# One half unit of the output projection moves behind the projection's last part

## The chip, the cores and the metric

The kernel runs on one core of one Trainium2 chip. The metric is the device time of one execution in microseconds (us), lower is better. Five engines work side by side, each through its own instructions in its own order: PE (TensorE, matmuls; PEld are its weight loads), DVE (VectorE), ACT (ScalarE), POOL (GpSimd) and SP (SyncE, which here only issues DMAs). They wait for each other through semaphores.

## What is computed

The reference is one step of a hybrid streaming encoder over 576 tokens (64 of a sample, 512 of a prompt) with a model width of 1024:

```
h   = x @ W_in                                  # q, k, v of 8 + 8 heads, and an indexer
mix = concat(ForgettingAttention(h_A), IndexedSparseAttention(h_B))
x   = LN1(alpha * x + mix @ W_o)
x   = LN2(alpha * x + relu(x @ W_up)^2 @ W_down)
x   = x + sigmoid(x @ W_g + b_g) * (p @ W_ple)
```

The change lies in the third line, `alpha * x + mix @ W_o` and the LN1 behind it. `mix` has 1024 rows (features), 128 for each of eight pairs of heads.

## The kernel before

Everything is kept with the features on the 128 partitions and the 576 tokens along the free dimension. The tokens are worked in two halves of 288, called A and B. Each fp32 product is made from three matmuls of 32-bit words that were split into a high and a low part (`gemm`, L282 to L292): 128x128 weights by 128x288 data, three for each block of 128 input rows. `BH` and `BL` hold the high and low parts of `mix`, and after LN1 those of its result.

**Stages around the change, in program order.** `wo1` (L1117) multiplies `mix` by `W_o` for pairs 0 to 5 (768 of the 1024 rows): eight units, one for each 128 output features, each with both halves: 18 matmuls (6 blocks by 3) for a half. While it runs, the attention of pairs 6 and 7 is still being made; its small steps come from a second generator, `ticks`, and `drive(wo1(), 46, ticks(9 + 7), 48)` deals them out: 48 small steps over the first 46 of 48 yields, a yield being 6 matmuls. The result of each unit goes to `Y` by one DVE instruction (L1135: `Y*ALPHA + product`). Then `wo2(A)` (L1306) adds what is missing, pairs 6 and 7, for half A: 48 matmuls, in four steps of two output blocks each; DVE adds each step to `Y` (L1335) and `ln.add` sums `Y` over the features for LN1 of half A. `wo2(B)` does the same for half B, another 48, but first copies `Y` into the accumulator with ACT (L1313), and takes the sum back with ACT (L1333). `ple` follows: 96 matmuls on data of its own (`pT`), evacuated by ACT (L1350). Then `up_first` multiplies LN1's result by `W_up`, half A first.

**LN1** (class `LayerNorm`) is a chain over three engines that is dealt out between these matmuls: DVE and POOL sum `Y` (L1186 to L1191; for half A all on DVE, for half B the adds of the second and third step on POOL and the last on DVE), PE forms the mean (L1208 for A, L1206 for B), DVE subtracts it (L1232, four pieces), ACT squares (L1234, L1237), DVE adds the squares (L1238, L1240), PE forms the variance (L1258 for A), ACT and DVE take its inverse root, PE spreads it (L68), and DVE and ACT scale and split into `BH` and `BL` (L1270, L1274, L1278).

**Weights** arrive by SP's DMAs in fp32 (`wraw`, four places in this stage), ACT casts the high part (L191), DVE subtracts to get the low part (L195); both go to `whl`, 6 places until `wo1` is over and 13 from then on. A place is free again after the last matmul that reads it. `WT.ahead(u)` forces a unit's pieces to be made at that point of the program; `unit_w(u, oldest)` says which units still hold their places.

**Order.** A scheduler places the program's instructions on each engine's list at build time. On the chip each list is worked through in order, so the order on the list is what the change moves.

**PSUM.** The accumulators `m` and `g` of these stages rotate through three places (`psum_g`, two in one pool and one in another). A place is reused when its evacuation has read it.

Of the kernel before, what the change touches and what calls it, by code (L numbers as in the profile page):

```python
# [11 lines left out]
OP = mybir.AluOpType  # L12
# [12 lines left out]
ALPHA = 2.0 ** 0.25  # L25
# [6 lines left out]
HW = NT // 2  # L32
# [4 lines left out]
def tile_hybrid_step(ctx: ExitStack, tc: tile.TileContext, I, O):  # L37
    nc = tc.nc
    PE, ACT, DVE, POOL, SP = nc.tensor, nc.scalar, nc.vector, nc.gpsimd, nc.sync
# [34 lines left out]
    def later(delay, fn):  # L74
        evq.append((clock[0] + delay, len(evq), fn))
# [16 lines left out]
    def drive(main, n_main, bg, n_bg, drain=True, close=True):  # L92
        done = 0
        for i, _ in enumerate(main):
            clock[0] += 1
            pop_due(POP)
            for fl in fillers:
                fl()
            while bg is not None and done * n_main < (i + 1) * n_bg:
                done += 1  # L100
                if next(bg, 0) == 0:
                    bg = None
                    break
        if close:
            flush()
        if bg is not None and drain:
            for _ in bg:
                pass
# [171 lines left out]
    WT = Weights()  # L280

    def gemm(ps, W, kmap, aH, aL, cols, yield_every=6, first=True, last=True, wc=slice(0, 128), k0=0, onto=False):  # L282

        n = len(kmap) * 3
        i = 0
        for kw, ka in enumerate(kmap, k0):
            for w, a in ((0, aH), (0, aL), (1, aH)):
                PE.matmul(ps, W(w, kw, wc), a[:, ka, cols], start=(first and i == 0 and not onto), stop=(last and i == n - 1),  # L288
                          skip_group_check=onto)
                i += 1  # L290
                if i % yield_every == 0:
                    yield 1  # L292
# [47 lines left out]
    U = {}  # L340
# [506 lines left out]
    def proj(p):  # L847
# [4 lines left out]
        for kind in "kqv" if p else "qv":  # L852
            u = U[kind, p]
            W = WT.use(u)
            WT.ahead(u + 1)
# [5 lines left out]
            for h in range(2):  # L861
                for _ in gemm(m[:, h, :HW], W, range(8), AH, AL, slice(h * HW, (h + 1) * HW)):
                    WT.step()
# [6 lines left out]
    BH = BL = None  # L870
# [139 lines left out]
    def job(t):  # L1010
        return all_jobs[t] if 0 <= t < len(all_jobs) else None

    def ticks(n):

        for _ in range(n):
            t = tick_no[0]
            tick_no[0] += 1
            for micro in PLAN:
                for stage, lag in micro:
                    for x in (1, 0) if stage in LATE else (0,):  # L1020
                        j = job(t - lag - x)
                        if not j or (stage in LATE and j["late"] != x):
                            continue
                        if (j["close"] or stage not in (pv, oevac)) and not (stage is make_bias and "bias" in j):
                            stage(j)
                yield 1
# [65 lines left out]
    for p in range(7):  # L1092
# [5 lines left out]
        if p == 5:  # L1098
            Y = base.tile([128, 8, NT], F32, name="Y", tag="Y")
# [17 lines left out]
    def wo1():  # L1117
        side = delayed(7, v_out(7))
        for j in range(8):
            u = U["o", j]  # L1120
            W = WT.use(u)
            WT.ahead(u + 1)
            m = psum_m()
            for h in range(2):
                if (j, h) == (7, 1):
                    WT.ahead(u + 2)
                for _ in gemm(m[:, h, :HW], W, range(6), BH, BL, slice(h * HW, (h + 1) * HW)):
                    WT.step()
                    if j < 3:
                        next(side, 0)  # L1130
                    yield 1
                if j in (5, 6) and h == 0:
                    p_split(j - 5)
            y = Y[:, j].rearrange("p (a c) -> p a c", a=2)
            later(0, lambda y=y, m=m: DVE.scalar_tensor_tensor(  # L1135
                y, y, ALPHA, m[:, :, :HW], op0=OP.mult, op1=OP.add))

    drive(wo1(), 46, ticks(9 + 7), 48)
    pPA.close()
    pA.close()  # L1140

# [9 lines left out]
    A, B = slice(0, HW), slice(HW, NT)  # L1151
# [4 lines left out]
    def psum_g():  # L1156
        turn[0] += 1
        if turn[0] % 3 == 2:
            return psB.tile([128, 2, 512], F32, name="g", tag="g", bufs=1)
        return psM.tile([128, 2, 512], F32, name="g", tag="m", bufs=2)  # L1160
# [4 lines left out]
    unit_w = WT.use  # L1165

    class LayerNorm:
# [54 lines left out]
        def steps(self):  # L1222
# [80 lines left out]
            for j in range(0, 8, 2):  # L1303
                bias(j)
                yield 1

    def wo2(hs, ln, steps):
        onto = hs is B

        def take(j):  # L1310
            m = psum_g()
            if onto:
                ACT.copy(m[:, :, :HW], Y[:, j:j + 2, hs])  # L1313
            return m

        ms = {0: take(0)}
        for j in range(0, 8, 2):
            m = ms[j]
            if onto and j < 6:
                ms[j + 2] = take(j + 2)  # L1320
            for x in range(2):
                cs = slice((j + x) * 128, (j + x + 1) * 128)
                for k in (6, 7):
                    W = unit_w(U["ok", k], U["ok", 6])
                    for _ in gemm(m[:, x, :HW], W, (0,), BH[:, k:k + 1], BL[:, k:k + 1], hs,
                                  first=(k == 6), last=(k == 7), wc=cs, onto=onto):
                        pass
                WT.step(steps)
                yield 1

            def ev(j=j, m=m):
                if onto:
                    ACT.copy(Y[:, j:j + 2, hs], m[:, :, :HW])  # L1333
                else:
                    DVE.tensor_tensor(Y[:, j:j + 2, hs], m[:, :, :HW], Y[:, j:j + 2, hs], OP.add)  # L1335
                ln.add(j)
            later(0, ev)
            if not onto and j < 6:
                ms[j + 2] = take(j + 2)

    def ple():
        for j in range(8):
            W = unit_w(U["ple", j // 4])
            m = psum_g()
            for h in range(2):
                for _ in gemm(m[:, h, :HW], W, (0, 1), PT2[:, :, 0], PT2[:, :, 1], slice(h * HW, (h + 1) * HW),
                              wc=slice((j % 4) * 128, (j % 4 + 1) * 128)):
                    WT.step(j >= 4)
                    yield 1
            later(0, lambda j=j, m=m: ACT.copy(PL[:, j].rearrange("p (a c) -> p a c", a=2), m[:, :, :HW]))  # L1350
            if j % 2:
                later(2, lambda j=j: SP.dma_start(PLD[:, (j - 1) * NT:(j + 1) * NT], PL[:, j - 1:j + 1].rearrange("p j t -> p (j t)")))

    def seq(*gens):
        for g in gens:
            yield from g
# [156 lines left out]
    L1B = LayerNorm(B, 0, (5, 9, 4, 0))  # L1513
    L1 = both(L1A, L1B)
    drive(wo2(A, L1A, 4), 8, None, 0)
    early = fb.tile([128, 4], F32, name="ln_r", bufs=2)
    ACT.activation(early[:, 0:1], epst, AF.Sqrt, bias=epst[:, 0:1])
    drive(seq(wo2(B, L1B, 0), ple()), 24, L1, 24, False)
    XS = sums_of_x()

    def first(n, gen):
# [153 lines left out]
```

## Time and profile before

| | |
|---|---|
| time, median of 3 runs | 759.03 us (758.97 to 759.3) |
| profiled execution: its time, its span | 758.77 us, 756.8 us |
| PE busy, DVE, ACT, POOL | 751.4, 563.9, 452.0, 115.4 us |
| 288.4 to 300 us (`wo2`): PE, DVE, ACT, POOL busy of 11.6 | 11.60, 10.38, 8.16, 1.01 us |
| 300 to 310 us (end of `wo2(B)`, `ple`), of 10 | 10.00, 9.58, 8.19, 1.86 us |
| 310 to 320 us (`ple`, `up_first`), of 10 | 10.00, 9.62, 10.00, 1.44 us |

A row of the timeline gives the start in us from the span's start, the duration, the engine, the line of the kernel, the operation and `out<-in` with the shape and `xcount`; in brackets stands how long the engine was idle before, and what ended that. A row with `x` and a count above 1 merges instructions that follow each other; its duration is that of all. Matmuls are pipelined: a row's duration is longer than the distance to the next matmul. The chain of waits is the sequence of work that ended last, followed back from the end; its rows give start, length, engine and line.

### The profile page before, as it was taken

What the parts mean: (1) busy time and instruction counts of PE and PEld (TensorE: products, weight loads), DVE (VectorE), ACT (ScalarE), POOL (GpSimd) and SP (SyncE); (2) the same over time, 40 slices, a digit from 0 to 9 for tenths busy, and PEclk for the clock granted to TensorE, in tenths of its full rate; (3) what the DMA queues carried; (4) which work ended last, traced back from release to release, by engine and by line L of the source; (5) the groups of instructions that cost most, each with busy time, mean ns of one, the idle gap of its engine ahead of it and who ended that gap; (6) DMA issues with size and microseconds to landing.
All of it is one profiled execution on the core that took longest, in us unless ns stands there. A gap on an engine that the chain in (4) does not pass through costs nothing.

```text
span 756.8 us, 15089 instructions
## 1 busy us (share of the span) xinstructions
PE 751.4 (99%) x5770; PEld 740.6 (98%) x5770; DVE 563.9 (75%) x1212; ACT 452.0 (60%) x952; POOL 115.4 (15%) x125
## 2 busy tenths in 40 slices
PE   9999999999999999999999999999999999999997
PEld 9999999999999999999999999999999999999997
DVE  7969898896567558999997776667766776658853
ACT  6687776789888537983474454444534455526551
POOL 7217445543310001000000000000000000011100
PEclk9999999999999999999999999999999999999999
DMA  8655768564546335411333322133322314630002
GB/s 295 197 133 153 180 197 221 150 238 129 154 162 207 112 121 192 154 61 60 104 117 108 106 89 82 59 112 92 105 66 76 112 56 132 225 132 29 29 29 69
DMA packets 42407, 95.38 MB, mean 126 GB/s; under 512 B 6224, under 2 KB 17232, under 8 KB 42208
## 3 DMA queue, kind: packets, MB, share of 16 engines
q1 hardware_dynamic: 41904, 94.14, 40.5%
q8 instruction: 45, 0.74, 0.4%
q10 hardware_dynamic: 432, 0.29, 0.1%
q14 instruction: 26, 0.21, 0.1%
HBM read 66.38 MB, written 9.54 MB: 100 GB/s over the span
## 4 chain that ended last, share of the span: by engine, by line
PE 99%; DVE 0%; ACT 0%; issue 0%; POOL 0%; DVEq 0%; ACTq 0%; POOLq 0%
PE g L288 58%; PE m L288 25%; PE n L288 3%; PE V L970 2%; PE S L898 1%; PE S L896 1%; PE T L68 1%; PE T L933 1%; PE S L447 1%; PE m L441 1%; PE m L447 1%; PE X L447 1%; PE V L311 0%; PE X L678 0%; PE S L888 0%; PE S L678 0%
## 5 line engine op out<-in xcount | busy, mean ns | idle before, releaser
L191 ACT CAST whl<-wraw 128x512 fp32r<-128x512 f32 (+1 forms) x212 | 127.8, 610 | 154.8 <-PE g L288 133.0
L195 DVE TENSOR_TENSOR whl<-wraw,whl 128x512 fp32r<-128x512 f32 (+1 forms) x194 | 131.0, 685 | 67.0 <-ACT whl L191 66.8
L288 PE MATMUL m<-AH,whl 128*128 128x288 f32 x736 | 175.4, 306 | 0.0
L288 PE MATMUL g<-BH,whl 128*128 128x288 f32 (+2 forms) x784 | 161.1, 294 | 0.0
L288 PEld LDWEIGHTS g<-BH,whl 128*128 128x128 f32 x784 | 127.3, 188 | 0.1
L288 PEld LDWEIGHTS m<-AH,whl 128*128 128x128 f32 x736 | 126.1, 188 | 1.2
L288 PE MATMUL g<-BL,whl 128*128 128x288 f32 (+2 forms) x392 | 115.3, 294 | 0.0
L288 PE MATMUL m<-AL,whl 128*128 128x288 f32 x368 | 109.0, 296 | 0.0
L288 PE MATMUL g<-hidO,whl 128*128 128x288 f32 (+2 forms) x768 | 103.4, 295 | 0.0
L288 PE MATMUL g<-hidE,whl 128*128 128x288 f32 (+2 forms) x768 | 103.4, 294 | 0.0
L288 PEld LDWEIGHTS g<-hidO,whl 128*128 128x128 f32 x768 | 102.3, 188 | 0.0
L288 PEld LDWEIGHTS g<-hidE,whl 128*128 128x128 f32 x768 | 102.2, 188 | 0.0
L288 PEld LDWEIGHTS g<-BL,whl 128*128 128x128 f32 x392 | 73.6, 188 | 0.1
L288 PE MATMUL g<-s,whl 128*128 128x288 f32 x504 | 71.2, 294 | 0.0
L1186 POOL TENSOR_TENSOR ln_s<-Y 128x576 f32<-128x576 f32 (+2 forms) x3 | 4.3, 1434 | 432.8 <-DVE Y L1504 362.7
L288 PEld LDWEIGHTS m<-AL,whl 128*128 128x128 f32 x368 | 69.4, 189 | 0.8
L288 PEld LDWEIGHTS g<-s,whl 128*128 128x128 f32 x504 | 68.1, 188 | 0.0
L910 ACT ACTIVATE sP<-sP,st 128x128 f32<-128x128 f32 (+4 forms) x72 | 39.5, 549 | 21.1 <-DVE st L906 20.7
L195 POOL TENSOR_TENSOR whl<-wraw,whl 128x512 fp32r<-128x512 f32 x34 | 44.3, 1304 | 24.9 <-ACT whl L191 23.3
L288 PE MATMUL m<-BH,whl 128*128 128x288 f32 x192 | 43.4, 303 | 0.0
L1480 DVE TENSOR_TENSOR Y<-Y,g 128x576 f32<-128x576 f32 x40 | 29.9, 749 | 14.5 <-PE g L288 14.5
L916 ACT ACTIVATE sP<-sP,st 128x128 f32<-128x128 f32 (+4 forms) x63 | 34.0, 549 | 8.3 <-DVE st L914 7.6
(288 smaller groups left out, 1283.1 us busy)
## 6 DMA issues: line engine op xcount, KB each, us to landing
wraw<-in_w_up_dram SPq DMA_DIRECT2D x32, 512.0 KB, 3.4
wraw<-in_w_down_dram SPq DMA_DIRECT2D x32, 512.0 KB, 3.4
wraw<-in_w_qkv_dram SPq DMA_DIRECT2D x23, 512.0 KB, 4.0
wraw<-in_w_gate_dram SPq DMA_DIRECT2D x8, 512.0 KB, 4.9
wraw<-in_w_o_dram SPq DMA_DIRECT2D x8, 384.0 KB
sR<-sP SPq DMA_DIRECT2D x10, 256.0 KB, 2.5
kE<-kh SPq DMA_DIRECT2D x16, 144.0 KB, 4.1
kO<-kh SPq DMA_DIRECT2D x16, 144.0 KB
```

Source lines behind the costliest of these rows:

```text
L68: PE.transpose(out, in_, ident[:n, :n])
L191: ACT.copy(self.hv[h][0], src)
L195: eng.tensor_tensor(lv, src, f(hv), OP.subtract)
L288: PE.matmul(ps, W(w, kw, wc), a[:, ka, cols], start=(first and i == 0 and not onto), stop=(last and i == n - 1), skip_group_check=onto)
L441: PE.matmul(mk[:, h, :HW], w0(part, k), a[:, k, h * HW:(h + 1) * HW], start=(k == 0 and i == 0), stop=(k == 7 and i == 2))
L447: PE.matmul(acc[b][:n[b], c], a[:, k, at[b]:at[b] + n[b]], ixw(part, k)[:, c], start=(k == 0 and i == 0), stop=(k == 7 and i == 2))
L896: PE.matmul(ps[:, :n], Q[:, d], K[:, NS:NS + n], start=True, stop=False)
L898: PE.matmul(ps[:, :n], Q[:, c], P["KL"][:, hh, :n], start=False, stop=True)
L910: ACT.activation(j["P"], j["P"], AF.Exp, bias=j["st"][:, 0:1], scale=-1.0, accum_out=j["st"][:, 2:3])
L916: ACT.mul(j["P"], j["P"], j["st"][:, 3:4])
L970: PE.matmul(P["O"][r, (i - 1) * 128 + c.start:(i + 1) * 128], P["vt"][:, kb, r], t[:, hh, kb, c], start=(kb == 0), stop=(kb == i))
L1480: later(0, lambda y=y, m=m: DVE.tensor_tensor(y, y, m[:, :, :HW], OP.add))
```

## The change

The eighth unit of `wo1` (output features 896 to 1023) now makes only half A. Its half B, 18 matmuls and a DVE instruction on 288 tokens instead of 576, is a new generator `wo1_last` that runs between `wo2(A)` and `wo2(B)`. The 48 small steps of `ticks` are dealt out over the first 43 of now 45 yields. The eighth unit's weights keep their two places in `whl` through `wo2(A)`. The pieces of unit `ok7` (the weights of pair 7 in `wo2`) are asked for one half unit earlier in the program, at the eighth unit's half A. The LN1 steps are dealt out over 27 yields instead of 24.

```diff
             m = psum_m()
-            for h in range(2):
-                if (j, h) == (7, 1):
+            for h in range(2 if j < 7 else 1):
+                if j == 7:
                     WT.ahead(u + 2)
                 for _ in gemm(m[:, h, :HW], W, range(6), BH, BL, slice(h * HW, (h + 1) * HW)):
                     WT.step()
...
             y = Y[:, j].rearrange("p (a c) -> p a c", a=2)
-            later(0, lambda y=y, m=m: DVE.scalar_tensor_tensor(
-                y, y, ALPHA, m[:, :, :HW], op0=OP.mult, op1=OP.add))
-
-    drive(wo1(), 46, ticks(9 + 7), 48)
+            n = 2 if j < 7 else 1
+            later(0, lambda y=y, m=m, n=n: DVE.scalar_tensor_tensor(
+                y[:, :n], y[:, :n], ALPHA, m[:, :n, :HW], op0=OP.mult, op1=OP.add))
+
+    drive(wo1(), 43, ticks(9 + 7), 48)
...
+    def wo1_last():
+
+        W = unit_w(U["o", 7], U["o", 7])
+        m = psum_g()
+        for _ in gemm(m[:, 0, :HW], W, range(6), BH, BL, B):
+            WT.step()
+            yield 1
+        y = Y[:, 7, B]
+        later(0, lambda: DVE.scalar_tensor_tensor(y, y, ALPHA, m[:, 0, :HW], op0=OP.mult, op1=OP.add))
...
-                    W = unit_w(U["ok", k], U["ok", 6])
+                    W = unit_w(U["ok", k], U["ok", 6] if onto else U["o", 7])
...
-    drive(seq(wo2(B, L1B, 0), ple()), 24, L1, 24, False)
+    drive(seq(wo1_last(), wo2(B, L1B, 0), ple()), 27, L1, 27, False)
```

Lines behind the new function have numbers that are higher by 11 (L1313, L1333 and L1335 become L1324, L1344 and L1346), those between L1135 and it by 1 (L1208 becomes L1209, L1258 becomes L1259).

**First place: DVE, from the second step of `wo2(A)` to the last sum before LN1's mean of half A.** The numbers tell the buffers apart: `g_` are the accumulators of `wo2`'s four steps, in order, `whl_` pieces of weights. Before:

```order
L195 TENSOR_TENSOR whl_4391<-wraw_4337,whl_4391 128x512
L195 TENSOR_TENSOR whl_4393<-wraw_4337,whl_4393 128x512
L1335 TENSOR_TENSOR Y_2907<-g_4359,Y_2907 128x2x288
L195 TENSOR_TENSOR whl_4407<-wraw_4351,whl_4407 128x512
L1186 TENSOR_TENSOR ln_s_4375<-Y_2907 128x2x288
L1335 TENSOR_TENSOR Y_2907<-g_4384,Y_2907 128x2x288
L1335 TENSOR_TENSOR Y_2907<-g_4409,Y_2907 128x2x288
L1188 TENSOR_TENSOR ln_s_4375<-ln_s_4375,Y_2907 128x2x288 x2
L1191 TENSOR_TENSOR ln_s_4375<-ln_s_4375 128x288
```

With the change (`wraw_4273` is the first unit of `W_up`, `wraw_4319` the second):

```order
L1346 TENSOR_TENSOR Y_2907<-g_4341,Y_2907 128x2x288
L195 TENSOR_TENSOR whl_4350<-wraw_4273,whl_4350 128x512
L195 TENSOR_TENSOR whl_4352<-wraw_4273,whl_4352 128x512
L1187 TENSOR_TENSOR ln_s_4357<-Y_2907 128x2x288
L1346 TENSOR_TENSOR Y_2907<-g_4366,Y_2907 128x2x288
L1346 TENSOR_TENSOR Y_2907<-g_4383,Y_2907 128x2x288
L1189 TENSOR_TENSOR ln_s_4357<-ln_s_4357,Y_2907 128x2x288
L195 TENSOR_TENSOR whl_4611<-wraw_4319,whl_4611 128x512
L1189 TENSOR_TENSOR ln_s_4357<-ln_s_4357,Y_2907 128x2x288
L1316 SCALAR_TENSOR_TENSOR Y_2907<-Y_2907,g_4403 128x288
L1192 TENSOR_TENSOR ln_s_4357<-ln_s_4357 128x288
```

A weight piece and the evacuation of the moved half unit (L1316) now stand ahead of the last sum of half A (L1192), and two weight pieces of the first `W_up` unit stand between the second step's evacuation and the first sum.

**Second place: ACT and DVE in `wo2(B)`, from the first step's copy back to the sum of A's squares.** ACT before, where `g_4429`, `g_4431`, `g_4445`, `g_4461` are the four steps of `wo2(B)`:

```order
L1333 COPY Y_2907<-g_4429 128x2x288
L1313 COPY g_4461<-Y_2907 128x2x288
L191 CAST whl_4605<-wraw_4351 128x512
L1333 COPY Y_2907<-g_4431 128x2x288
L191 CAST whl_4666<-wraw_4366 128x512
L1333 COPY Y_2907<-g_4445 128x2x288
L1234 ACTIVATE ln_s_4375<-Y_2907 128x2x288
L1237 ACTIVATE ln_sq_4482<-Y_2907 128x2x288
L1237 ACTIVATE ln_sq_4494<-Y_2907 128x2x288
L1333 COPY Y_2907<-g_4461 128x2x288
```

ACT with the change, where the four steps are `g_4422`, `g_4424`, `g_4443`, `g_4467`:

```order
L1344 COPY Y_2907<-g_4422 128x2x288
L1324 COPY g_4467<-Y_2907 128x2x288
L1235 ACTIVATE ln_s_4357<-Y_2907 128x2x288
L191 CAST whl_4664<-wraw_4333 128x512
L1238 ACTIVATE ln_sq_4454<-Y_2907 128x2x288
L1238 ACTIVATE ln_sq_4464<-Y_2907 128x2x288
L1344 COPY Y_2907<-g_4424 128x2x288
L1344 COPY Y_2907<-g_4443 128x2x288
L1238 ACTIVATE ln_sq_4478<-Y_2907 128x2x288
L1344 COPY Y_2907<-g_4467 128x2x288
```

The copies back of the second and third step stood ahead of A's first square; now they stand behind A's third. POOL's two adds for half B read what these copies write. DVE before (`ln_s_4375` is the sum of A, `ln_s_4454` that of B):

```order
L1232 TENSOR_TENSOR Y_2907<-Y_2907,n_4471 128x2x288 x4
L1238 TENSOR_TENSOR ln_s_4375<-ln_s_4375,ln_sq_4482 128x2x288
L195 TENSOR_TENSOR whl_4666<-wraw_4366,whl_4666 128x512
L1238 TENSOR_TENSOR ln_s_4375<-ln_s_4375,ln_sq_4494 128x2x288
L1188 TENSOR_TENSOR ln_s_4454<-ln_s_4454,Y_2907 128x2x288
L1238 TENSOR_TENSOR ln_s_4375<-ln_s_4375,ln_sq_4504 128x2x288
L1191 TENSOR_TENSOR ln_s_4454<-ln_s_4454 128x288
L1240 TENSOR_TENSOR ln_s_4375<-ln_s_4375 128x288
```

DVE with the change (`ln_s_4357` is A, `ln_s_4452` is B):

```order
L1233 TENSOR_TENSOR Y_2907<-Y_2907,n_4439 128x2x288 x4
L1239 TENSOR_TENSOR ln_s_4357<-ln_s_4357,ln_sq_4454 128x2x288
L195 TENSOR_TENSOR whl_4664<-wraw_4333,whl_4664 128x512
L1239 TENSOR_TENSOR ln_s_4357<-ln_s_4357,ln_sq_4464 128x2x288
L1239 TENSOR_TENSOR ln_s_4357<-ln_s_4357,ln_sq_4478 128x2x288
L1189 TENSOR_TENSOR ln_s_4452<-ln_s_4452,Y_2907 128x2x288
L1241 TENSOR_TENSOR ln_s_4357<-ln_s_4357 128x288
L1192 TENSOR_TENSOR ln_s_4452<-ln_s_4452 128x288
```

B's last add (L1189, which takes POOL's sum) now stands directly ahead of A's last sum (L1241); before, one of A's adds and B's last sum stood between them.

**Third place: PE, from the last matmuls of `wo2(B)` to the middle of `ple`** (`pT` matmuls are `ple`; L1258 and L1259 the variance of A; L1206 and L1207 the mean of B). Before:

```order
L288 MATMUL g<-BL,whl 128x288
L288 MATMUL g<-BH,whl 128x288
L288 MATMUL g<-pT,whl 128x288 x36
L1258 MATMUL n<-onesm,ln_s 128x1 x3
L1206 MATMUL n<-ln_hl,onesr 128x288
L288 MATMUL g<-pT,whl 128x288 x6
L1206 MATMUL n<-ln_hl,onesr 128x288
L288 MATMUL g<-pT,whl 128x288 x6
L68 MATMUL n<-ident,ln_r 128x128 x3
L288 MATMUL g<-pT,whl 128x288 x48
```

With the change:

```order
L288 MATMUL g<-BL,whl 128x288
L288 MATMUL g<-BH,whl 128x288
L288 MATMUL g<-pT,whl 128x288 x18
L1259 MATMUL n<-onesm,ln_s 128x1 x3
L288 MATMUL g<-pT,whl 128x288 x14
L68 MATMUL n<-ident,ln_r 128x128 x3
L288 MATMUL g<-pT,whl 128x288 x4
L1207 MATMUL n<-ln_hl,onesr 128x288 x2
L288 MATMUL g<-pT,whl 128x288 x60
```

The variance of A stands 18 matmuls earlier than before. The mean of A (L1208, now L1209) has moved too: it stood behind 30 of `wo2(B)`'s 48 matmuls, and now stands behind 13.

## The prediction

> **What bounds the kernel now.** I read the page first, then who waited for whom on PE, then the chain of waits, then the timelines of PE, DVE, ACT and POOL between 278 and 326 us. The page:
>
> ```profile
> span 756.8 us, 15089 instructions
> PE   9999999999999999999999999999999999999997
> PEclk9999999999999999999999999999999999999999
> ```
>
> PE is busy in every slice, at the full granted clock. Busy rows of pipelined matmuls can hide slow issue, so the next two views matter more: PE's waits, and pieces of the chain.
>
> ```profile
> PE V L311 <- POOL ones L59: 1.0, 1, 1.0
> ...
> 288.44 10.31 PE g L288 x78
> 298.75 0.48 PE n L1208 x2
> 299.24 7.16 PE g L288 x54
> 306.40 0.74 PE n L1258 x6
> ...
> 319.66 57.00 PE g L288 x430
> ```
>
> PE waits once, at the very start. In the stage of the change it issues 78 matmuls in 10.31 us and 54 in 7.16, 0.132 us each, and 430 in 57.00 far behind it, 0.133 each: the stage already runs at the pace of the rest. So the end is set by PE's sum of matmuls. The change leaves that sum as it is. What it can win is what PE loses in this stage today, and that is at most the two LN1 rows together, 0.48 + 0.74 = 1.2 us if they cost nothing at all, and more likely 0.1 to 0.2 us. What it can lose has no such bound: any instruction on PE's list that comes before its data holds all matmuls behind it.
>
> **The change part by part.**
>
> *The moved matmuls.* 18 leave `wo1` and 18 come behind `wo2(A)`: 18 x 0.132 = 2.4 us removed, 2.4 us added, nothing. One DVE instruction on 576 tokens becomes two on 288. DVE is off the path except where PE waits for it, below.
>
> *Pair 7's steps dealt out denser.* The last attention job before `wo2`:
>
> ```profile
> 265.45 0.49 PE L888 MATMUL S<-KcT,QB 128*128 128x192 f32 x2
> 267.79 3.15 SPq L925 DMA_DIRECT2D sR<-sP  x2
> 278.18 0.28 PE L933 MATMUL T<-identr,sR 128*128 128x128 f32 x2
> ```
>
> Its scores are made at 265.45, its last DMA is issued by 270.94, and PE transposes the result at 278.18. By the order, 72 instead of 84 projection matmuls stand between the first and the last of these rows, so 12 x 0.132 = 1.6 us of some 7 go. Even a landing of 3.4 us (the row of the weights, below) leaves about 2 us. I cost it at nothing; the work that hides it is `wo1` itself. Between pair 7's output and `wo2(A)` there are still 30 matmuls.
>
> *What goes to ACT, DVE and SP's list.* The weight unit `ok7` needs the two places of the seventh unit's weights. That unit is now unfinished when pair 7's output is made, so the order puts `ok7`'s two subtractions behind pair 7's evacuation. Before, they were done ahead of it:
>
> ```profile
> 281.70 0.68 DVE L195 TENSOR_TENSOR whl<-wraw,whl 128x512 fp32r<-128x512 f32 x1
> 284.70 0.69 DVE L993 TENSOR_TENSOR BL<-V,BH 128x512 fp32r<-128x512 f32 x1 [2.32 <-ACT BH L992]
> 286.41 2.50 DVE L195 TENSOR_TENSOR whl<-wraw,whl 128x512 fp32r<-128x512 f32 x4
> 288.94 0.76 DVE L1135 SCALAR_TENSOR_TENSOR Y<-Y,m 128x576 f32<-128x576 f32 x1
> 282.41 6.25 SPq L169 DMA_DIRECT2D wraw<-in_w_up_dram  x4
> wraw<-in_w_up_dram SPq DMA_DIRECT2D x32, 512.0 KB, 3.4
> wraw<-in_w_gate_dram SPq DMA_DIRECT2D x8, 512.0 KB, 4.9
> 288.28 0.29 PE L288 MATMUL g<-BH,whl 128*128 128x288 f32 x1
> ```
>
> SP issued the DMA of the first `W_up` unit at 282.41, as the last of those subtractions ended at 282.38. Now it follows `ok7`'s second piece: pair 7's evacuation comes 2.4 us earlier (284.70 becomes 282.3), then one piece of `ple`, the small evacuations, `ok7`'s first piece, the seventh unit's evacuation and `ok7`'s second piece: about 1.7 + 0.61 + 0.67 + 0.61, so it ends near 286.0. The DMA is 3.6 us later and lands 3.4 us (by the row's median) to 4.9 us (by the slowest weights) after its issue, 289.4 to 290.9. PE does not need this unit before `up_first`, 25 us later. But DVE's list has its two pieces ahead of LN1's sums.
>
> *First wait: the mean of half A.* `wo2(A)` starts at 288.28 - 2.4 = 285.9. The mean stood on PE at 298.59; 17 matmuls earlier is 296.35.
>
> ```profile
> 298.59 0.65 PE L1208 MATMUL n<-ln_s,onesm 128*128 128x288 f32 x2
> 294.02 1.54 DVE L1335 TENSOR_TENSOR Y<-g,Y 128x576 f32<-128x576 f32 x2
> 297.05 0.46 DVE L1191 TENSOR_TENSOR ln_s<-ln_s 128x288 f32<-128x288 f32 x1
> ```
>
> DVE had its sum ready at 297.51, 1.1 us before PE asked. Now (first place of the order) the `W_up` pieces start near 290.1, then come 2 pieces at 0.61 (2.50 / 4), a sum, two evacuations and a sum at 0.67 each, which gives 294.0. The next piece reuses a place of the moved half unit, free after its ninth matmul: 285.9 + 57 x 0.132 + 0.2 = 293.6, plus a cast of 0.6, so it starts at 294.3. Then 0.61 + 0.67 + 0.45 + 0.46 give 296.5. With the slowest landing everything is up to 1.1 us later. PE's wait here is 0.15 to 1.2 us; I take 0.35, near the median landing.
>
> *Second wait: the variance of half A.* I count from the mean M.
>
> ```profile
> 299.28 2.75 DVE L1232 TENSOR_TENSOR Y<-Y,n 128x576 f32<-128x576 f32 x4 [0.23 <-PE n L1208]
> 301.94 0.97 DVE L1238 TENSOR_TENSOR ln_s<-ln_s,ln_sq 128x576 f32<-128x576 f32 x1
> 303.44 0.74 DVE L1238 TENSOR_TENSOR ln_s<-ln_s,ln_sq 128x576 f32<-128x576 f32 x1
> 305.81 0.45 DVE L1240 TENSOR_TENSOR ln_s<-ln_s 128x288 f32<-128x288 f32 x1
> 298.23 0.64 ACT L1333 COPY Y<-g 128x576 f32<-128x576 f32 x1
> 301.20 1.25 ACT L1237 ACTIVATE ln_sq<-Y 128x576 f32<-128x576 f32 x2
> 298.99 1.43 POOL L1186 TENSOR_TENSOR ln_s<-Y 128x576 f32<-128x576 f32 x1 [70.13 <-ACT Y L1333]
> 300.86 1.43 POOL L1188 TENSOR_TENSOR ln_s<-ln_s,Y 128x576 f32<-128x576 f32 x1 [0.43 <-ACT Y L1333]
> 301.48 4.92 PE L288 MATMUL g<-pT,whl 128*128 128x288 f32 x36
> 306.31 0.83 PE L1258 MATMUL n<-onesm,ln_s 128*128 128x1 f32 x6
> ```
>
> PE's own position: from the mean at 298.59 to `ple` at 301.48 it took 2.89 us for 18 matmuls, that is 2.38 and 0.51 beside them. Now 35 and then 18 matmuls stand between: 53 x 0.132 + 0.51 = M + 7.5. The data: the first subtraction starts 0.69 behind the mean and takes 0.69 a piece; ACT's first square starts at M + 1.5, and a cast and two squares (0.57 each) follow, so the copy back of `wo2(B)`'s second step, which the change put behind them, starts at M + 3.7 and ends at M + 4.35. POOL starts 0.12 later (298.99 after 298.87) and its two adds take 1.43 each: M + 7.4. B's last add on DVE waits for them (0.67), and A's last sum stands behind it (0.45): M + 8.55. Before, POOL was through at 302.29 and B's add came at 304.10, without a wait. That is a wait of 1.0 us on PE even if POOL runs freely.
>
> It does not. DVE adds with both inputs in SBUF and POOL adds get in each other's way:
>
> ```profile
> 692.05 1.56 POOL L1186 TENSOR_TENSOR ln_s<-Y 128x640 f32<-128x640 f32 x1 [9.36 <-DVE Y L1504]
> 701.38 1.90 POOL L1188 TENSOR_TENSOR ln_s<-ln_s,Y 128x640 f32<-128x640 f32 x1 [7.77 <-DVE Y L1504]
> 701.16 0.68 DVE L195 TENSOR_TENSOR whl<-wraw,whl 128x512 fp32r<-128x512 f32 x1
> 702.50 1.33 DVE L195 TENSOR_TENSOR whl<-wraw,whl 128x512 fp32r<-128x512 f32 x1
> ```
>
> POOL's add at 701.38 came into a DVE piece that ended at 701.84 and took 0.34 longer than its like; the DVE piece at 702.50 came into that add, which ended at 703.28, and took 0.65 longer. The add at 301.94 above took 0.23 longer under POOL's second add. Each time the second one ran its full length after the first, but for some 0.12 us. With the change three such DVE instructions, the piece and two adds of squares, fall into POOL's 2.9 us. One after the other: piece until M + 4.7, POOL's first add from 4.6 to 6.0, DVE's add 5.9 to 6.6, POOL's second 6.5 to 7.9, DVE's next 7.8 to 8.5, then B's add 0.67 and A's sum 0.45: M + 9.65, or M + 9.9 with DVE's two adds ahead of POOL's second. The wait is 2.15 to 2.4 us; bounds 1.0 (they overlap freely) and 2.4. I take 2.25, since every meeting in this trace was a full wait.
>
> [...]
>
> *Further on.* The inverse root (L68) has 14 `ple` matmuls and the variance's 0.74 us as cover, 2.6 us. DVE needs for a sum, two pieces, a subtraction and a reciprocal 0.37 + 1.2 + 0.43 + 0.15 = 2.2. No wait. `up_first` finds LN1 ready as before:
>
> ```profile
> 313.79 0.51 DVE L1278 SCALAR_TENSOR_TENSOR BL<-Y,gb,BH 128x288 fp32r<-128x288 f32 x1
> 315.61 0.29 PE L288 MATMUL g<-BH,whl 128*128 128x288 f32 x1
> ```
>
> The first pair was complete 1.3 us ahead of PE; with the change the variance comes at 296.7 + 9.8 = 306.5, about when it came before (306.31), and PE reaches `up_first` later, so this cover grows. It is cover, though, and buys nothing.
>
> *Sum.* 0 + 0.35 + 2.25, less 0.1 for small waits of today that may vanish: +2.5 us, against the profiled execution's 758.77 us (span 756.8 and 2.0 around it): 761.3. The median of the runs is 0.26 above that execution, so 761.5. A measurement of this kernel cannot tell less than about 0.2%, 1.5 us, from no change.
>
> **The rivals.**
>
> *The data fit* (14%): not slower. The order's position for the variance is right, since POOL's sum is there when DVE gets to it. That needs POOL's two adds over by M + 6.3 instead of M + 7.4. For it: before, PE's position met the data within 0.1 us (306.31). Against it: POOL's 1.43 us, twice, and a start that the order ties to ACT's squares. Time: 759.0, between 758.7 and 759.4.
>
> *POOL alone* (20%): the adds overlap with DVE, the wait is 1.0 instead of 2.25. Sum 0.35 + 1.0 - 0.1 = 1.25 us, 760.3. About three in ten of this case lie above 1.5 us.
>
> *Later still* (8%): the `W_up` unit lands after 4.9 us, the mean is 1.2 us late, and `up_first`, whose accumulators are freed by a crowded ACT (10.0 of 10 us busy from 310 to 320), adds some tenths: +3.6 us, 762.6, up to 763.
>
> *Faster* (3%): more than 1.5 us would have to go, and only 1.2 us of LN1's matmul rows stand there.
>
> **How the numbers follow.** Both waits as worked out, 55%: 761.5, own range 760.9 to 762.1. Slower: 55 + 8 + 6 (of *POOL alone*) = 69%. Within 0.2%: 14 + 14 = 28%. Faster: 3%. The range 759.4 to 762.8 leaves out most of *the data fit*, the far end of *later still* and *faster*.
>
> **What would show it.** In the changed kernel's waits, PE has rows for L1259 on DVE's L1241 (about 2 us) and L1209 on L1192 (some tenths), and PE idles in the slice near 304 to 307 us; DVE's L1189 waits for POOL, POOL's L1189 or DVE's L1239 beside it lasts longer than alone; the first `W_up` DMA is issued near 286. Behind 320 us nothing differs but a shift. I am wrong if PE shows no wait at L1259, if the copy back of the second step comes ahead of A's squares, or if the time is lost or won outside 285 to 320 us.

## The result, and the profile after

| | before | with the change |
|---|---|---|
| median, us | 759.11 (758.97 to 759.30, 4 runs) | 763.53 (762.12 to 764.06, 4 runs) |
| profiled execution: time, span, us | 758.77, 756.8 | 762.12, 760.1 |

The ratio is 1.0054, 95% interval 1.0041 to 1.0067: 4.4 us slower, above the forecast of 761.5 us and above its range (759.4 to 762.8). The four executions lie far apart, and the profiled one is the fastest of them. Its page and PE's waits:

```profile
span 760.1 us, 15087 instructions
PE   9999999999999999899999999999999999999997
PEclk9999999999999999999999999999999999999999
```

```profile
PE n L1259 <- DVE ln_s L1241: 1.9, 1, 1.9
```

One slice lost its 9, and a new row names the wait: half A's variance on its last sum of squares. A piece of the chain of waits of the same execution, then the timelines of PE, DVE, ACT and POOL:

```profile
296.81 0.74 PE n L1209 x2
```

```profile
306.50 0.83 PE L1259 MATMUL n<-onesm,ln_s 128*128 128x1 f32 x6 [1.92 <-DVE ln_s L1241]
307.19 2.10 PE L288 MATMUL g<-pT,whl 128*128 128x288 f32 x14
...
310.25 4.00 PE L288 MATMUL g<-pT,whl 128*128 128x288 f32 x29
```

```profile
300.24 0.76 DVE L1239 TENSOR_TENSOR ln_s<-ln_s,ln_sq 128x576 f32<-128x576 f32 x1
...
301.51 3.90 DVE L1239 TENSOR_TENSOR ln_s<-ln_s,ln_sq 128x576 f32<-128x576 f32 x2
305.34 0.75 DVE L1189 TENSOR_TENSOR ln_s<-ln_s,Y 128x576 f32<-128x576 f32 x1
306.00 0.45 DVE L1241 TENSOR_TENSOR ln_s<-ln_s 128x288 f32<-128x288 f32 x1
```

```profile
299.46 1.25 ACT L1238 ACTIVATE ln_sq<-Y 128x576 f32<-128x576 f32 x2
300.62 1.16 ACT L1344 COPY Y<-g 128x576 f32<-128x576 f32 x2
```

```profile
301.37 1.51 POOL L1187 TENSOR_TENSOR ln_s<-Y 128x576 f32<-128x576 f32 x1 [72.20 <-ACT Y L1344]
302.96 1.83 POOL L1189 TENSOR_TENSOR ln_s<-ln_s,Y 128x576 f32<-128x576 f32 x1
```

The mean M starts at 296.81 and the variance at 306.50, M + 9.7. POOL starts at M + 4.6, behind ACT's copies back, which come at M + 3.8, behind A's third square. Two of DVE's adds of squares take 3.90 us under POOL's adds, where one alone takes 0.76; they end behind POOL, at 305.4, B's add and A's sum follow, and PE has been idle for 1.9 us.

How much of the profiled difference is the change's? An instruction of the attention and the last sigmoid of the gate, from the timelines of before:

```profile
200.91 0.69 DVE L993 TENSOR_TENSOR BL<-V,BH 128x512 fp32r<-128x512 f32 x1 [1.16 <-ACT BH L992]
...
752.53 0.68 ACT L1577 ACTIVATE relu<-g,gb 128x192 f32<-128x192 f32 x2 [2.99 <-PE g L288]
```

And the same two with the change:

```profile
201.22 0.69 DVE L993 TENSOR_TENSOR BL<-V,BH 128x512 fp32r<-128x512 f32 x1 [1.16 <-ACT BH L992]
...
755.87 0.68 ACT L1588 ACTIVATE relu<-g,gb 128x192 f32<-128x192 f32 x2 [2.99 <-PE g L288]
```

At 200 us, where both programs still have the same order, this execution is already 0.31 us late; at the end it is 3.34 late. So 3.0 us arise in between. Measured from the start of the matmul ahead, less the usual 0.132 us, PE loses 2.07 at the variance (2.205 from start to start; the profile, which goes by modelled ends, says 1.9), 0.16 at the mean (0.295) and about 0.3 at half B's variance near 322 us; some 0.5 us are small pieces whose cause I leave open. That is near the 2.5 us of the prediction, in part by luck: the last two of these were not in its sum, and this execution escaped what the others lost. The median lost 4.4. The difference between the two is what the first experiment had to find.

### The profile page after: what moved, and what is told of

The parts are those of the page before. It is cut to its first block, busy times and chain, and to the rows that moved or that the text cites. A ratio compares the mean times of both kernels' runs of the same rounds, so it can differ in the third digit from the quotient of the medians.

```text
span 760.1 us, 15087 instructions
## 1 busy us (share of the span) xinstructions
PE 752.7 (99%) x5770; PEld 741.1 (97%) x5770; DVE 565.2 (74%) x1213; ACT 452.1 (59%) x952; POOL 115.5 (15%) x125
## 4 chain that ended last, share of the span: by engine, by line
PE 92%; DMA 3%; DVE 2%; ACT 2%; issue 1%; SPq 0%; DVEq 0%; ACTq 0%
PE g L288 56%; PE m L288 24%; PE n L288 3%; PE V L970 2%; DMA wraw<-in_w_qkv_dram 2%; PE S L898 1%; PE S L896 1%; PE T L68 1%; PE T L933 1%; DMA iraw<-in_w_idx_dram 1%; DVE whl L195 0%; ACT BH L1275 0%; ACT PL L1361 0%; PE X L678 0%; DVE Y L1233 0%
## 5 line engine op out<-in xcount | busy, mean ns | idle before, releaser
L288 PE MATMUL g<-BH,whl 128*128 128x288 f32 (+2 forms) x796 | 163.6, 294 | 0.0
L288 PEld LDWEIGHTS g<-BH,whl 128*128 128x128 f32 x796 | 129.4, 188 | 0.2
L288 PE MATMUL g<-BL,whl 128*128 128x288 f32 (+2 forms) x398 | 117.3, 295 | 0.0
L288 PE MATMUL m<-BH,whl 128*128 128x288 f32 x180 | 41.0, 303 | 0.0
```

## The experiments

All kernels were timed against the kernel before on the same chip; "before" below is the median of those runs.

| kernel | median, us | before, us | ratio (95% interval) | PE's wait near the variance, us | its executions |
|---|---|---|---|---|---|
| `again` (the change) | 763.67 | 759.35 | 1.0059 (1.0047 to 1.0071) | 1.9 | 761.93, 763.6 to 765.7 |
| `twice` | 765.74 | 759.07 | 1.0089 (1.0075 to 1.0102) | 3.3 | 765.5 to 766.1 |
| `before_x3` | 763.24 (763.14 without the one of 1036 us) | 759.12 | 1.0054 (1.0041 to 1.0068) | not profiled at the place | 762.4 to 764.6 |
| `before_x3_again` | 762.76 | 759.44 | 1.0045 (1.0031 to 1.0058) | 2.2 | 762.7 to 764.0 |
| `before_x2` | 760.02 | 759.12 | 1.0011 (1.0002 to 1.0020) | 0.9 | 759.6 to 760.3 |
| `adds_dve` | 760.08 | 759.35 | 1.0010 (1.0001 to 1.0018) | none | 759.6 to 760.3 |
| `one_pool` | 760.78 | 759.07 | 1.0021 (1.0012 to 1.0030) | 1.0 | 760.3 to 761.2 |
| `var_later` | 761.23 | 759.35 | 1.0027 (1.0016 to 1.0037) | none there, 1.0 at L1207 | 761.1 to 761.8 |
| `lnA_later` | 758.99 | 759.12 | 0.9998 (0.9989 to 1.0007) | none | 758.7 to 759.5 |
| `dense_only` | 760.64 | 759.35 | 1.0015 (1.0006 to 1.0024) | 0.8 | 759.8 to 761.2 |
| `undense` | 762.51 | 759.07 | 1.0041 (1.0029 to 1.0054) | 1.1 | 760.76, 762.3 to 763.2 |
| `undense_dve` | 759.31 | 759.07 | 1.0003 (0.9994 to 1.0012) | none | 758.6 to 759.7 |

### Where the rest of the median goes

**The changed kernel once more**, no edit:

> The changed kernel once more, for another profiled execution. Theory: in every execution PE waits about 2.1 us at L1259 for L1241 and some tenths at L1209 and L1207, about 2.7 us together; what an execution takes beyond 761.8 us has its place before 60 us (where both programs have the same order) or is a stretch with a granted clock below full speed. Rival 1: PE's idle 2 us near 305 us costs clock behind it, so a profiled execution of over 763 us shows a lower PEclk in the slices behind 306 us and matmuls further apart than 0.132 us there, 1 to 2 us in all. Rival 2: in a longer execution the wait at L1259 itself is longer, 3 to 4 us, because the transfer of the first W_up unit lands later. Median of the rounds expected 763 to 764 by each.

The new profiled execution took 763.69 us, 1.6 us more than the first one. Its PE timeline, then its table by stretches (PE busy and count, then PEld, DVE, ACT, POOL; the number behind POOL is the granted clock, the share of TensorE's full clock that it was given in the stretch), then its waits:

```profile
306.59 0.83 PE L1259 MATMUL n<-onesm,ln_s 128*128 128x1 f32 x6 [1.91 <-DVE ln_s L1241]
307.28 2.86 PE L288 MATMUL g<-pT,whl 128*128 128x288 f32 x14
...
311.89 2.28 PE L288 MATMUL g<-pT,whl 128*128 128x288 f32 x16
```

```profile
306.00:312.00 6.00, 5.41 (x30) 5.39 (x31) 4.32 (x11) 1.56 (x4) 0.00 (x0) 0.72 0.41 137
312.00:320.00 8.00, 8.00 (x63) 8.00 (x62) 6.84 (x15) 8.00 (x17) 1.44 (x1) 1.00 0.40 160
```

```profile
PE n L1209 <- DVE ln_s L1192: 0.4, 1, 0.4
```

The same stretch in the first execution of the changed kernel:

```profile
306.00:312.00 6.00, 5.50 (x43) 5.50 (x44) 5.40 (x14) 3.15 (x7) 0.00 (x0) 1.00 0.44 158
```

The wait is the same 1.9 us. Behind it the same 14 matmuls took 2.86 us instead of 2.10, and PE got through 30 instructions in the six microseconds instead of 43, at a granted clock of 0.72. From 308.3 us to 311.7 us the matmuls of `ple` start 0.240 us apart instead of 0.132. From the variance to the first matmul of `ple` behind half B's mean PE takes 5.30 us (306.59 to 311.89) where the first execution took 3.75 (306.50 to 310.25): 1.55 us more. On the page all this is invisible: the row PEclk shows a 9 in every slice, since a slice is 19 us long. The wait for the mean is longer too, 0.52 us from start to start instead of 0.16 (0.4 in the row above), but up to that place this execution had been earlier by 0.26. Rival 1 holds; rival 2, a longer wait, does not hold here. (The longest execution, 765.67 us at a clock of 0.994, was not profiled.) Of the ten executions of the changed kernel, eight had a mean clock of 0.994 to 0.998 and took 763.07 us or more, and two, at 1.0, took 761.93 and 762.12.

**A longer wait, with the order kept:**

```diff
-                (DVE if self.sl is A else POOL).tensor_tensor(self.s, y[:, 0:2], y[:, 2:4], OP.add)
+                [(DVE if self.sl is A else POOL).tensor_tensor(self.s, y[:, 0:2], y[:, 2:4], OP.add) for _ in range(2 if self.sl is B else 1)]
```

> The change, with half B's first add on POOL done twice (the same sum, written again): 1.4 to 1.8 us more on POOL; up to 350 us the order on every engine is that of the changed kernel. Theory: PE's wait at L1259 grows by as much, to 3.4 to 4.0 us, and now every execution loses granted clock behind it, so the time is that of the change's slower executions plus the longer wait: 765 to 766.5 median, clock 0.994 to 0.998 in each, matmuls 0.24 us apart for 3 us or more. Rival (the lower clock has nothing to do with the idle time): executions with clock 1.0 stay as frequent as with the change, median 764.8 to 765.3 only. Rival (POOL does not set the wait): no change against 763.6.

All five executions were in 765.5 to 766.1, at clocks of 0.994 to 0.996. Its PE timeline and two stretches:

```profile
307.74 1.44 PE L1259 MATMUL n<-onesm,ln_s 128*128 128x1 f32 x6 [3.29 <-DVE ln_s L1241]
```

```profile
306.00:312.00 6.00, 4.26 (x18) 4.26 (x19) 3.73 (x8) 1.34 (x3) 0.53 (x1) 0.58 0.26 81
312.00:318.00 6.00, 6.00 (x42) 5.98 (x41) 4.50 (x10) 3.82 (x8) 0.00 (x0) 0.85 0.29 116
```

The wait grew by 1.4 us, and now no execution escapes. POOL sets the wait, and the slow stretch grows with it.

**The same wait in the kernel before, without the change** (the edit above with 3 in the place of 2):

> The kernel before, without any part of the change, with half B's first add on POOL done three times (the same sum written again): about 3 us more on POOL ahead of B's add, A's last sum and the variance on PE; the order of the other engines is as before up to 350 us. Theory (an idle PE of about 2 us costs its own length and then granted clock): a wait of 1.8 to 2.6 us at L1258, in most executions matmuls 0.24 us apart for some 3 us behind it and a mean clock of 0.996 to 0.998, time 761.8 to 763.2. Rival (the lower clock belongs to something else in the change): the wait alone, clock 0.999 to 1.0 in all executions, 760.8 to 761.8.

The profiled execution had a granted clock of 0.656 from its start on, long before it reached the edit, and took 1036 us; it says nothing here and is not in the figures. The other four took 762.4 to 764.6 us at clocks of 0.996 to 0.998. The same kernel once more, for its profile:

> The kernel before with half B's first add on POOL done three times, once more, because the profiled execution of the last look had a granted clock of 0.656 from its start on and shows nothing of the place. Theory: PE waits 1.8 to 2.6 us at L1258 for L1240, and behind it, not elsewhere, matmuls stand 0.24 us apart for some 3 us; the loss behind the wait is 1.3 to 1.6 us; median 762.4 to 763.6 with clocks of 0.996 to 0.998. Rival (the clock is lost elsewhere, or not by the idle time): PEclk below full speed in other slices, or none.

PE's timeline and the table by stretches of that run:

```profile
308.73 1.18 PE L1258 MATMUL n<-onesm,ln_s 128*128 128x1 f32 x6 [2.18 <-DVE ln_s L1240]
```

```profile
296.00:306.00 10.00, 10.00 (x76) 9.89 (x76) 8.85 (x11) 8.87 (x16) 6.61 (x4) 1.00 0.18 55
306.00:312.00 6.00, 3.82 (x20) 3.58 (x19) 4.42 (x9) 1.23 (x3) 0.00 (x0) 0.75 0.52 175
312.00:318.00 6.00, 6.00 (x35) 5.98 (x34) 4.49 (x9) 4.68 (x9) 1.43 (x1) 0.68 0.27 109
318.00:350.00 32.00, 32.00 (x243) 31.89 (x242) 31.12 (x52) 28.86 (x56) 0.00 (x0) 1.00 0.26 88
```

Full clock ahead of the wait, 0.75 and 0.68 behind it, full clock again from 318 us. Nothing of the change is in this kernel; the idle time alone brings the slow stretch, here a double one. All nine executions in the comparison were at 0.996 to 0.998.

**A shorter wait in the kernel before** (2 in the place of 3):

> The kernel before with half B's first add on POOL done twice. Theory: a wait of 0.3 to 1.0 us at L1258, too short for the clock (dense_only and one_pool, with gaps of 1.13 and 1.25 us, kept it in 20 of 21 executions, undense with 1.40 us lost it in 4 of 5): time 759.4 to 760.2, clock 0.999 to 1.0. Rival (any wait can cost the clock): some executions 1.4 us longer than the others.

The wait was 0.9 us, and eleven executions lay within 0.7 us of each other at 0.999 to 1.0. The time is the wait and no more: + 0.9 us.

### What makes the wait

**Half B's adds off POOL**, both:

```diff
-                (DVE if self.sl is A else POOL).tensor_tensor(self.s, y[:, 0:2], y[:, 2:4], OP.add)
+                (DVE if self.gi == 0 else POOL).tensor_tensor(self.s, y[:, 0:2], y[:, 2:4], OP.add)
             else:
-                (DVE if j == 6 or self.sl is A else POOL).tensor_tensor(self.s, self.s, y[:, j:j + 2], OP.add)
+                (DVE if j == 6 or self.gi == 0 else POOL).tensor_tensor(self.s, self.s, y[:, j:j + 2], OP.add)
```

> The change, with LN1's two adds of half B (second and third step) on DVE instead of POOL. Theory: POOL's 2 x 1.4 to 1.8 us and the blocking of DVE under them go; DVE's own list up to A's last sum grows by two adds, 1.4 us, one of them behind A's sum, so that A's sum ends near M + 7.9 to 8.2 where PE asks at M + 7.9 (the order puts 21 instead of 18 matmuls of ple ahead): wait 0 to 0.4 us, time 759.2 to 760.3. Rival (ACT's late copy back of half B's steps sets the end, not POOL): the wait stays at 1.0 us or more, time 761 or more.

DVE's list at the same place, with two adds more on it:

```profile
301.29 0.75 DVE L1239 TENSOR_TENSOR ln_s<-ln_s,ln_sq 128x576 f32<-128x576 f32 x1
...
302.62 0.76 DVE L1239 TENSOR_TENSOR ln_s<-ln_s,ln_sq 128x576 f32<-128x576 f32 x1
...
303.96 0.46 DVE L1241 TENSOR_TENSOR ln_s<-ln_s 128x288 f32<-128x288 f32 x1
```

Both adds of squares are back at 0.75 us, and A's sum comes 1.8 us earlier, counted from the mean (M + 7.4, M being 296.59 here, instead of M + 9.2), although DVE does more. PE does not wait. The theory holds, with 0.7 us over the kernel before.

**Only the second add off POOL** (the second of the two edited lines above):

> The change with only the second of half B's adds on DVE, the first left on POOL. One add on POOL, started when ACT's copy back is through, M + 4.5, ends near M + 6; by the order B's two adds stand ahead of A's sum on DVE and PE asks behind 21 matmuls of ple, M + 7.9. Theory: one meeting of POOL and DVE is left, A's sum ends near M + 8.0 to 8.8; wait 0.1 to 0.9 us, time 759.7 to 760.8, clock at 1.0. Rival (the copies back of ACT set the end): the wait stays over 1.5 us, time over 762.

DVE and POOL where they meet:

```profile
302.00 1.99 DVE L1239 TENSOR_TENSOR ln_s<-ln_s,ln_sq 128x576 f32<-128x576 f32 x1
```

```profile
301.87 1.52 POOL L1187 TENSOR_TENSOR ln_s<-Y 128x576 f32<-128x576 f32 x1 [72.20 <-ACT Y L1344]
```

One meeting is left. DVE's add comes 0.13 us into POOL's, and POOL's ends at 303.39; 0.75 us run behind it would end at 304.14, and DVE's ended at 303.99. So it waited POOL's add out, but for some 0.15 us. PE's wait of 1.0 us is a little more than expected. Ten executions, none at a lower clock.

**PE asks later:**

```diff
-    L1A = LayerNorm(A, 0, (4, 5, 2, 8))
+    L1A = LayerNorm(A, 0, (4, 8, 2, 8))
```

> The change, with three more steps of waiting ahead of half A's variance (waits 4, 8, 2, 8): on PE the variance stands behind 36 matmuls of ple again instead of 18, 2.4 us later; ahead of it ACT, DVE and POOL keep the order of the changed kernel, so that POOL's two adds still run under DVE's adds. Theory: the loss is PE's place for the variance alone; its data come at M + 9.7 and PE asks at M + 9.9, so the wait at L1259 goes to 0 to 0.3 us and the time is 759.2 to 760.2. Rival (the crowded lists cost by themselves, or what is late by 2.4 us is missed by up_first): a wait of 1 to 2 us appears at the inverse root or ahead of up_first, time 761 to 763.

PE's waits:

```profile
PE n L1207 <- DVE ln_hl L1200: 1.0, 2, 0.7
```

The wait at the variance is gone, as the theory said, but the time is 1.9 us over before, in the rival's range, though not where the rival looked: PE now waits for half B's mean and later for its variance. PE's place alone was not the cause: the data of both halves are late.

**LN1 of half A as late as the moved matmuls:**

```diff
-    L1A = LayerNorm(A, 0, (4, 5, 2, 8))
+    L1A = LayerNorm(A, 0, (7, 5, 2, 8))
```

> The whole change with LN1 of half A three steps later (waits 7, 5, 2, 8), so that its mean and squares stand where they stood against wo2(B) before the change: ACT's copies back of half B's second and third step come ahead of A's squares again, POOL keeps its two adds, the denser steps stay. Theory (ACT's late copies start POOL's late adds): POOL starts early again and the wait falls from 2.1 to about that of the denser steps alone, 0.9 to 1.2 us, because two weight pieces stand ahead of A's subtraction here too; no lower clock; time 760.2 to 761.0. Rival (the order of ACT's copies is not the cause): wait 2 us, 763 or more. Rival (it is all of the cause): no wait, 759.2 to 759.8.

PE, ACT, DVE and POOL of this kernel:

```profile
301.37 4.94 PE L288 MATMUL g<-pT,whl 128*128 128x288 f32 x36
306.19 0.83 PE L1259 MATMUL n<-onesm,ln_s 128*128 128x1 f32 x6
```

```profile
298.39 0.63 ACT L1344 COPY Y<-g 128x576 f32<-128x576 f32 x1
...
299.97 0.64 ACT L1344 COPY Y<-g 128x576 f32<-128x576 f32 x1 [0.42 <-PE g L288]
300.50 0.69 ACT L1235 ACTIVATE ln_s<-Y 128x576 f32<-128x576 f32 x1
```

```profile
305.69 0.45 DVE L1241 TENSOR_TENSOR ln_s<-ln_s 128x288 f32<-128x288 f32 x1
```

```profile
299.15 1.44 POOL L1187 TENSOR_TENSOR ln_s<-Y 128x576 f32<-128x576 f32 x1 [70.41 <-ACT Y L1344]
300.74 1.44 POOL L1189 TENSOR_TENSOR ln_s<-ln_s,Y 128x576 f32<-128x576 f32 x1
```

The whole loss is gone: the ratio is 0.9998. The moved matmuls, the denser steps and POOL's adds are all still there. ACT copies back ahead of its squares, POOL starts at 299.15 instead of 301.37 (0.7 us behind the mean of half A instead of 4.6) and runs undisturbed (1.44 us an add), and A's sum is ready at 306.14, when PE asks. The rival that expected no wait is right, and my theory, which kept 1 us for the denser steps, is not. The edit moves the whole chain of half A, though: ACT's order changes with it, and so do the places of A's mean and variance on PE, where the variance stands behind 36 matmuls of `ple` again. `var_later` shows that PE's place is not enough; the order of ACT's copies was not changed by itself. What had gone wrong is a count: LN1's steps wait in yields, the change put three yields of `wo1_last` ahead of `wo2(B)`, and so half A's chain came three yields early against `wo2(B)`'s evacuations.

### The two parts of the change alone

**The denser steps alone**, in the kernel before:

```diff
-    drive(wo1(), 46, ticks(9 + 7), 48)
+    drive(wo1(), 43, ticks(9 + 7), 48)
```

> The kernel before with pair 7's steps dealt out over 43 instead of 46 yields, and nothing else. Theory: no wait on PE from it, time as before within 0.2 us (758.9 to 759.4). Rival (part of the loss is in the attention steps, where the last transpose waits for its DMA): 0.3 to 1.5 us slower, with a PE wait between 255 and 282 us.

It is 1.3 us slower, yet not where the rival looked. PE's waits, and the timelines of DVE and POOL:

```profile
PE n L1258 <- DVE ln_s L1240: 0.8, 1, 0.8
```

```profile
282.78 0.69 DVE L993 TENSOR_TENSOR BL<-V,BH 128x512 fp32r<-128x512 f32 x1 [4.89 <-ACT BH L992]
...
299.89 1.55 DVE L195 TENSOR_TENSOR whl<-wraw,whl 128x512 fp32r<-128x512 f32 x1 [1.85 <-ACT whl L191]
301.36 2.73 DVE L1232 TENSOR_TENSOR Y<-Y,n 128x576 f32<-128x576 f32 x4
```

```profile
299.47 1.42 POOL L1186 TENSOR_TENSOR ln_s<-Y 128x576 f32<-128x576 f32 x1 [70.15 <-ACT Y L1333]
```

DVE stands idle for 4.89 us before pair 7's evacuation (2.32 in the kernel before), with the seventh unit's evacuation and weight pieces behind it on its list. What is pushed back there returns 17 us later (the steps in between, through SP's and ACT's lists, were not followed one by one): a weight piece that was over at 299.04 before (298.35 and 0.69 us) waits for its cast until 299.89, comes 0.42 us into POOL's first add and takes 1.55 us instead of 0.69. LN1's subtraction stands behind it and starts at 301.36 instead of 299.28 (this execution was already 0.46 us late at 200 us), and the variance waits. PE lost nothing in the attention itself.

**The move with less dense steps:**

```diff
-    drive(wo1(), 43, ticks(9 + 7), 48)
+    drive(wo1(), 45, ticks(9 + 7), 48)
```

> The move of the half unit with the attention steps dealt out over 45 yields instead of 43, so without the denser steps of pair 7. By the order, A's last sum of squares (L1241) now stands ahead of B's add that waits for POOL (L1189), with a weight piece ahead of it; PE still asks behind 18 matmuls of ple. Theory (DVE's queue behind POOL is what costs, and the denser steps brought it about): POOL's adds still block one or two of DVE's adds of squares, A's sum ends near M + 7.6 to 8.5 instead of M + 9.7, PE waits 0.2 to 1.0 us at L1259 and perhaps some tenths for half B's mean; no lower clock behind it; time 759.6 to 761.0. Rival (the move alone costs it, as the prediction had it with the denser steps at nothing): wait of 2 us and a time of 763 to 764 as with the whole change.

DVE and PE of this kernel:

```profile
281.77 0.75 DVE L1136 SCALAR_TENSOR_TENSOR Y<-Y,m 128x576 f32<-128x576 f32 x1
...
284.65 0.69 DVE L993 TENSOR_TENSOR BL<-V,BH 128x512 fp32r<-128x512 f32 x1 [1.53 <-ACT BH L992]
```

```profile
305.91 0.83 PE L1259 MATMUL n<-onesm,ln_s 128*128 128x1 f32 x6 [1.11 <-DVE ln_s L1241]
306.60 3.35 PE L288 MATMUL g<-pT,whl 128*128 128x288 f32 x14
```

The wait is 1.1 us, 0.8 less than with the whole change and just over what the theory expected. The theory missed the clock: four of five executions were at 0.998 and took 1.5 to 2.4 us more than the fifth. Those four lie 3.5 us over the kernel before in the middle, those of the whole change 4.3: the same 0.8.

**The same with half B's adds on DVE** (both edits):

> The move without the denser steps and with half B's adds on DVE. Theory: no wait at the variance; what is left is the mean of half A (0.1 to 0.2 us) and the mean of half B; time 759.2 to 760.1, no better than the kernel before, since PE's list has the same matmuls and little idle time to win. Rival (the move frees something that the waits hid): 758.3 or less.

As expected: no wait, 759.31 us, not to be told from the kernel before. Against `adds_dve`, with the denser steps, that is 0.5 us less over its own kernel before (0.24 against 0.73), inside the two intervals.

## Why the prediction was wrong, point by point

*What bounds the kernel*: right. Every loss that was traced is PE idle or PE at a lower clock.

*The moved matmuls*: right, nothing. `lnA_later` keeps the move and costs nothing.

*Second wait*: right in place, chain and size. It was put at M + 9.65 and came at M + 9.7; 2.07 us against 2.25. ACT's copy behind A's squares (undone in `lnA_later`), POOL's late adds and DVE blocked under them (undone in `adds_dve`) are shown by these two, the first together with the rest of A's chain, which that edit moves as a whole. *POOL alone* falls: two adds of 0.76 took 3.90 us. In `one_pool` the one add of squares that came under POOL's add took 1.99 us, where one alone takes 0.75. *The data fit* falls with 1.9 us of waiting.

*First wait*: 0.16 and 0.52 us in two executions, against 0.35; without the denser steps (`undense`) there was none. *The first `W_up` unit* landed when it was expected, 289.4 to 290.9; ACT's cast of it waited in the changed kernel:

```profile
289.89 1.14 ACT L191 CAST whl<-wraw 128x512 fp32r<-128x512 f32 x2 [1.58 <-DMA wraw<-in_w_up_dram]
```

*Denser steps at nothing*: wrong. I looked at their own transfer and at PE there, and found cover for both, rightly. I did not follow the things that stand behind pair 7 on DVE's list; that the seventh unit is late I put down to the move, and it was the denser steps: without them DVE evacuated that unit at 281.77 (`undense`), ahead of pair 7. Alone they cost 1.3 us; within the change, 0.8 us of the wait; with A's chain moved (`lnA_later`), nothing.

*Further on, no wait; behind 320 us only a shift*: almost. Half B's variance lost about 0.3 us near 322.

***Sum***: this is the step that failed. "0 + 0.35 + 2.25, less 0.1" ends when PE starts again, and the kernel does not. In eight of ten executions the granted clock was lower than in the other two, and in the one of the eight that was profiled the idle PE of 1.9 us is followed by 3.4 us at half clock, which take 1.55 us more. No rival held it either, so the range ended at 762.8. With this term the sum is 2.5 + 1.55, that is 4.05 us in such an execution, 763.1 us; the medians of 763.5 and 763.7 have some tenths more, of the size of what was lost at half B's variance and in the small pieces. The trace of before could not show it: there PE waits once, at the start.

## What to carry to other kernels

Where work is put into a loop that deals out a background chain by counts of steps, move the chain's counts with it: three yields were put ahead here, and three in the chain's first wait took the whole loss back. Price a wait on a busy TensorE twice, by its length and by a half-clock stretch behind it (next section: here none in 32 executions with waits of 0.8 to 1.0 us, 1.55 us more in `again` behind a wait of 1.9 us), and look for that stretch in windows of a few microseconds: in slices of 19 us the page showed nothing of a single stretch, and an 8 among the 9s for a double one. Run such a kernel several times, since one execution can escape. A denser background step is free only when what stands behind it on the other engines' lists has been followed too.

## What the runs showed of the hardware that was not expected

In these runs PE's waits of up to 1.0 us cost no granted clock, longer ones did in most executions. Sorted by the wait that the profile gives:

| PE's wait, us | kernel | executions with a slow stretch |
|---|---|---|
| 0.8 | `dense_only` | none of 11 |
| 0.9 | `before_x2` | none of 11 |
| 1.0 | `one_pool` | none of 10 |
| 1.1 | `undense` | 4 of 5 |
| 1.9 | the change, both runs | 8 of 10 |
| 2.2 | `before_x3`, both runs | 9 of 9 |
| 3.3 | `twice` | 5 of 5 |

(Counted by time and mean clock together: one execution of `dense_only` at 0.998 was no longer than the others.) The stretch comes in one length or its double. From the tables by windows: 6 us at 0.72 lose 1.68 us of clock in `again`, 3.4 us at half; `twice` loses 6 x (0.42 + 0.15) = 3.4 and `before_x3_again` 6 x (0.25 + 0.32) = 3.4, that is 6.8 us at half.

The traces record when the granted clock changed. In `again` it goes to 0.50 at 308.32 us and back to 1.00 at 311.73, 3.41 us later. In the kernel before, 1.00 is recorded from 4.93 to 755.86 us and in the first profile of the change from 5.08 to 759.43, which is 220 and 221 times 3.413 us; both times 0.50 follows, behind PE's last matmul (752.45 and 755.79). Counted from such changes in steps of 3.413 us, each of these traces falls into windows. Some of them, near the variance and at the end of the kernel, where PE has nothing left to do:

| kernel, start of the window, us | PE idle in it, us | idle or in the variance's matmuls, us | clock in the next window |
|---|---|---|---|
| `twice`, 757.49 | 1.49 | 1.49 | 1.00 |
| `dense_only`, the whole wait | 0.84 | 1.53 | 1.00 (306 to 318 us) |
| `before_x3_again`, 756.19 | 1.69 | 1.69 | 1.00 |
| the change, first profile, 305.46 | 1.05 | 1.74 | 1.00 |
| `undense`, 303.63 | 1.11 | 1.80 | 0.50 |
| the change, `again`, 304.90 | 1.69 | 2.38 | 0.50 |
| `twice`, 303.52 | 2.48 | 2.48 | 0.50 |
| `before_x3_again`, 305.63 | 2.18 | 2.50 | 0.50 |
| the kernel before, 752.45 | 3.41 | 3.41 | 0.50 |

By idle time alone these rows have no order: 1.69 us kept the clock once and lost it once, and 1.11 lost it. They have one when the time of the variance's matmuls, which write a single column each, is added (third column): full clock behind 1.49 to 1.74 us, half clock behind 1.80 us and more. What makes the clock go down, and whether another kernel would lose it at the same place, these rows do not show. The third column also parts the two profiles of the change. A boundary cuts the same wait into 0.87 and 1.74 us in the first, at 305.46, and leaves 2.38 in one window in `again`, where it falls at 304.90, 0.22 us into the wait. That the place of the boundary decides which executions are hit is my estimate from these two. Why the stretch lasts two windows in `twice` and `before_x3_again` stays open.
